# Attention's reciprocal sums through DRAM and a multiplication on GpSimd

## The chip, the core and the metric

The kernel runs on one core of a Trainium2 chip. The core has engines that run beside each other, each in its own fixed order: TensorE (PE, matmuls and transposes; PEld is its loading of weights), VectorE (DVE), ScalarE (ACT), GpSimd (POOL) and SyncE (SP). An instruction that waits holds up all that stands behind it on its engine. PE writes to PSUM, eight banks of 512 numbers in each of 128 partitions; DVE and ACT read it. DMA transfers are issued by an engine's queue (here SP and POOL above all) and then run by themselves.

The metric is the device time of one execution in microseconds (us): the median of 3 runs of the kernel before is 2940.63 us (2940.21 to 2942.37).

## The reference

Two layers over 1024 latent tokens and 256 context tokens of width 1024, in float32: a convolution module, then grouped-query attention, each followed by a SwiGLU network. The change touches the attention of the second layer alone. It has 16 heads of 64 numbers, and 4 heads of keys and values, each shared by 4 query heads; latent tokens read all 1280 tokens:

```python
def gqa_sdpa(q, k, v):
    B, Q, H, Dh = q.shape
    qg = q.reshape(B, Q, N_KV_HEADS, KV_GROUP, Dh)
    s = jnp.einsum("bqkgd,bskd->bkgqs", qg, k).astype(jnp.float32) * (Dh ** -0.5)
    p = jax.nn.softmax(s, axis=-1).astype(v.dtype)
    o = jnp.einsum("bkgqs,bskd->bqkgd", p, v)
    return o.reshape(B, Q, H * Dh)
```

The output of all heads is then multiplied by the matrix wo (the output projection), normalised, and added to the stream.

## The kernel before

Everything is laid out with features in the partitions and tokens in the free dimension. Products that need float32 accuracy are made of three matmuls: weights and inputs are each split into a rounded high part and the rest, the low part (`split`, L158 to L164: ACT copies the high part at L161, DVE subtracts at L164).

Attention is cut into 32 **units**: 4 key heads (t) times 8 blocks of 128 queries (qt); a unit has 4 query heads. The first 16 units are the first half of the tokens, the last 16 the second half.

- `scores` (L1105): for each of the 4 heads, 6 matmuls (L1116) give 128 x 1280 scores in PSUM; DVE scales them and takes the extreme (L1122); ACT takes the exponential in SBUF and adds up its row sums (L1124). There is room for two heads' scores in PSUM where attention runs alone, for one elsewhere.
- `values` (L1128): for each of 10 blocks of 128 keys, PE transposes the four heads' probabilities (L1134), ACT casts them to a high part (L1137), DVE subtracts the low part (L1138), and two matmuls (L1140, L1141) add them up in one PSUM bank, "av". Then DVE takes the reciprocals of the sums (L1145, 128 queries x 4 heads); POOL spreads each over 64 columns (L1147); ACT copies and DVE adds the two parts of the output (L1151, L1152); PE turns the spread reciprocals so that queries lie in the free dimension (L1155, two transposes into the next "av" bank, which is the same one, bank 7); DVE multiplies (L1156); POOL stores the result to the DRAM tile `od` (L1450). The last unit of each half is kept in SBUF (`olast`) and not stored.
- `attn_stream` (L1160) writes a unit's scores and the values of the unit before it in turns, as a generator. A unit's q is loaded by POOL one unit ahead (`load_q`, L1102), the keys of a head by POOL (`load_k`, L1095).

`attention` (L1430) writes the first half's units, at the start beside the projections of the last queries, then alone. The second half's stream goes into a background queue (`bgq`), and `pump` writes as much of it as its credit allows: during the output projection of the first half 0.4 of each step's us, during the first pass of the feed-forward network 0.95. `out_proj` (L1481) allocates the input tile o, loads it from `od` with four DMAs (L1485), splits it (L1489 to L1491), and then makes eight output tiles of 24 matmuls (L172 to L174).

The order on each engine is not the order of the code: a scheduler arranges the instructions by priority, which rises with the place in the code; `later` gives an instruction a later place. Buffers come from pools; where a tile gets the tag of an earlier one, it waits until that one was last used. "T" in the profile's rows stands for the tiles with the tags T1 to T6.

Of the kernel before, what the change touches and what calls it, by code (L numbers as in the profile page):

```python
# [8 lines left out]
F32 = mybir.dt.float32  # L9
# [3 lines left out]
ALU = mybir.AluOpType  # L13
AX = mybir.AxisListType

P = 128
# [4 lines left out]
TOK = CTX + SEQ  # L21
# [3 lines left out]
NH, NKV, HD = 16, 4, 64  # L25
# [30 lines left out]
class Kern:  # L56
# [1071 lines left out]
    def values(self, t, Ps, sums, dst, done):  # L1128
        nc, c = self.nc, self.c
        av = self.bank("av")  # L1130
        for j in range(NJ):
            tp = self.bank("pt")
            for h in range(4):
                nc.tensor.transpose(tp[:, h * P:(h + 1) * P], Ps[h][:, j * P:(j + 1) * P], c["ident"])  # L1134
            ph, pl = self.ptring[self.ptslot % len(self.ptring)]
            self.ptslot += 1
            nc.scalar.copy(ph, tp)  # L1137
            nc.vector.tensor_tensor(pl, tp, ph.bitcast(F32), op=ALU.subtract)  # L1138
            with self.later(self.lav):
                nc.tensor.matmul(av, lhsT=self.value(t, j), rhs=ph, start=j == 0, stop=False)  # L1140
                nc.tensor.matmul(av, lhsT=self.value(t, j), rhs=pl, start=False, stop=j == NJ - 1)  # L1141
            yield 0.87

        r = sums[:, 1, :]
        nc.vector.reciprocal(r, sums[:, 0, :])  # L1145
        rx = self.sb(256)
        nc.gpsimd.tensor_copy(rx.rearrange("p (h d) -> p h d", d=HD), r.unsqueeze(2).to_broadcast([P, 4, HD]))  # L1147
        tmp = self.sb(256).rearrange("p (a q) -> p a q", q=P)
        v = av.rearrange("p (a b q) -> p a b q", b=2, q=P)
        for b, r, o in ((0, slice(0, 64), slice(64, 128)), (1, slice(64, 128), slice(0, 64))):  # L1150
            nc.scalar.copy(tmp[r], v[o, :, b, :])  # L1151
            nc.vector.tensor_tensor(dst[r], v[r, :, b, :], tmp[r], op=ALU.add)  # L1152
        rb = self.bank("av")
        for a in range(2):
            nc.tensor.transpose(rb[:, a * P:(a + 1) * P], rx[:, a * P:(a + 1) * P], c["ident"])  # L1155
        nc.vector.tensor_tensor(dst, dst, rb[:, 0:256].rearrange("p (a q) -> p a q", q=P), op=ALU.mult)  # L1156
        done()
        yield 0.1

# [270 lines left out]
    def attention(self, final, qr):  # L1430
        nc, a, c = self.nc, self.a, self.c
        kbuf = self.T("T3", [P, 2 * TOK], F32R)
        pr1 = self.T("T1", [P, 3, TOK])
        prh = self.T("HS", [P, 4, TOK])
        ptt = self.T("T2", [P, 4, 2, 512], F32R)
        self.ptring = [(ptt[:, i, 0], ptt[:, i, 1]) for i in range(4)]
# [6 lines left out]
        def dst(q0):  # L1443
            def of(t, q):
                if (t, q % 4) == (NKV - 1, 3):
                    return self.olast, lambda: None
                st = self.sb(256).rearrange("p (a q) -> p a q", q=P)

                def done():
                    nc.gpsimd.dma_start(self.od[:, 2 * t:2 * t + 2, q * P:(q + 1) * P], st)  # L1450
                return st, done
            return of
# [11 lines left out]
        pr4 = None  # L1464
        for us in self.attn_stream(units, (self.kub, kbuf), dst(0), True):
            if self.bgq:
                self.pump(self.rate * us)
            elif pr4 is None:
                pr4 = self.T("T5", [P, 3, TOK])
                self.pring = self.pring[:4] + [pr4[:, 0], pr4[:, 1], pr4[:, 2]] + self.pring[4:]  # L1470
                self.set_banks(**alone)
                self.sring = [0, TOK]
# [8 lines left out]
        def out_proj(q0, otag, tags, ytag, box, xtag):  # L1481
            o = self.T(otag, [P, KT, 512])
            for q in range(4):
                n = 512 if q < 3 else 3 * P
                nc.gpsimd.dma_start(o[:, 2 * q:2 * q + 2, :n], self.od[:, 2 * q:2 * q + 2, q0:q0 + n])  # L1485
            oh = self.T(tags[0], [P, KT, 512], F32R)
            ol = self.T(tags[1], [P, KT, 512], F32R)
            for k in range(KT - 2):
                self.split(oh[:, k, :], ol[:, k, :], o[:, k, :])  # L1489
            self.split(oh[:, KT - 2:, :3 * P], ol[:, KT - 2:, :3 * P], o[:, KT - 2:, :3 * P])  # L1490
            self.split(oh[:, KT - 2:, 3 * P:], ol[:, KT - 2:, 3 * P:], self.olast)  # L1491
            yield 12
            y = self.T(ytag, [P, KT, 512])
            yacc = self.acc(512)
            box.append((y, yacc))

            xr = self.T(xtag, [P, KT if q0 else KT + 1, 512])
            last = self.T("HV", [P, 512]) if q0 else xr[:, KT, :]
            for q in range(0, KT, 2):
                nc.gpsimd.dma_start(xr[:, q:q + 2, :], self.x2d[:, q:q + 2, CTX + q0:CTX + q0 + 512])  # L1500
            more = [self.acc(512), last]
            box += [more, xr]
            for k in range(KT):
                o = self.bank("mm")
                self.proj(o, a["wo"][k], self.pairs(oh, ol), 512)
                nc.scalar.copy(y[:, k, :], o)  # L1506
                self.sq_acc(yacc, y[:, k, :], k)
                g = self.col[1][0][1][:, k:k + 1]
                w, p = (self.sm(512) for _ in range(2)) if k else more
                nc.scalar.activation(w, y[:, k, :], AF.Square, scale=g)  # L1510
                nc.vector.scalar_tensor_tensor(out=p, in0=y[:, k, :], scalar=g, in1=xr[:, k, :],
                                               op0=ALU.mult, op1=ALU.mult)
                if k:
                    for m, t in zip(more, (w, p)):
                        nc.vector.tensor_tensor(m, m, t, op=ALU.add)
                yield 5.1
        yL, yR, fL, fR, zL, zR = [], [], [], [], [], []
        for us in out_proj(0, "HS", ("T6", "T3"), "T4", yL, "HS"):
            self.pump(0.4 * us)
# [6 lines left out]
        def tail_R():  # L1526
            self.set_banks(mm=[0, 1, 2, 3], st=[5, 6])
            yield from out_proj(512, "T1", ("T2", "T5"), "T1", yR, "HR")
            yield from self.post_pre2(yR, self.xv[1], self.bank("st"), self.x3d[:, :, 512:], ("T2", "T5"), fR, True)
# [21 lines left out]
        yacc, n = self.acc(CTX), CTX  # L1551
# [172 lines left out]
```

## Time and profile before

The profiled execution took 2938.98 us, of which 2937.2 lie between its first and last instruction (the span).

| | us | share of the span | instructions |
|---|---|---|---|
| span of the profiled execution | 2937.2 | | 42731 |
| the profiled execution's own time | 2938.98 | | |
| median of 3 runs | 2940.63 | | |
| PE busy | 2847.7 | 97% | 16462 |
| DVE busy | 2160.7 | 74% | 3746 |
| ACT busy | 1335.5 | 45% | 2229 |
| POOL busy (with its DMA issues) | 222.6 | 8% | 377 |

Attention's values run from 1588.5 us (the first transpose of L1134) to 2393.7 us (the last multiplication of L1156). A row of a group names line, engine, operation, out<-in, the count, then the busy time and the mean duration in ns, and behind the second bar the idle time of the engine just before these instructions with what ended it. A row of a timeline has start, duration, engine and line; where it was idle before, the last bracket says how long and what it waited for. The chain is followed back from the last instruction, at each step to what released it.

### The profile page before, as it was taken

To read this page: it belongs to the slowest core of one execution; us is meant where nothing else is said; L and a number is where in the kernel's file an instruction comes from. 1 tells how busy PE (TensorE), PEld (TensorE's weight loads), DVE (VectorE), ACT (ScalarE), POOL (GpSimd) and SP (SyncE) were. 2 spreads that over 40 slices of the span, in tenths; PEclk is the share of its full clock that TensorE was granted. 3 is DMA by queue.
4 is the path that set the end of the run, shared out by engine and by line. 5 is a ranking of instruction groups with operands and counts; after the bars stand their busy time and mean duration, and the time that the engine had idled before them with its cause. 6 is when DMAs were issued, how large, how long until landed. Compare 5 with 4: busy or idle time off the path is not lost.

```text
span 2937.2 us, 42731 instructions
## 1 busy us (share of the span) xinstructions
PE 2847.7 (97%) x16462; PEld 2446.1 (83%) x16462; DVE 2160.7 (74%) x3746; ACT 1335.5 (45%) x2229; POOL 222.6 (8%) x377
## 2 busy tenths in 40 slices
PE   7999989999999999999999999989999999999998
PEld 6888877888888889989888787767777778889997
DVE  6887788847556378877786899786666666786777
ACT  5222255532222245544445688645555543444444
POOL 0000001011022001000011111110000000010000
PEclk9999999999999999999999999999999999999999
DMA  6443444334356224333345211322222143353332
GB/s 249 140 120 98 116 131 145 135 116 143 115 175 198 65 74 165 114 104 112 109 156 170 88 46 46 97 87 81 66 73 83 60 149 99 110 170 104 102 98 75
DMA packets 131755, 336.58 MB, mean 115 GB/s; under 512 B 31328, under 2 KB 52864, under 8 KB 130656
## 3 DMA queue, kind: packets, MB, share of 16 engines
q1 hardware_dynamic: 78016, 222.33, 24.1%
q0 software_dynamic: 29344, 103.83, 10.7%
q10 hardware_dynamic: 24192, 7.70, 1.1%
q8 instruction: 129, 2.11, 0.3%
q14 instruction: 74, 0.61, 0.1%
HBM read 289.50 MB, written 38.93 MB: 112 GB/s over the span
## 4 chain that ended last, share of the span: by engine, by line
PE 86%; DVE 7%; ACT 2%; issue 2%; DMA 2%; ACTq 0%; POOL 0%; SPq 0%; DVEq 0%; POOLq 0%
PE ps L172 15%; PE ps L173 15%; PE ps L174 15%; PE ps L875 4%; PE ps L877 4%; PE ps L876 4%; PE ps L1116 4%; PE ps L1134 4%; PE ps L1140 2%; PE ps L454 2%; PE ps L455 2%; PE ps L456 2%; PE ps L1141 2%; PE ps L185 1%; PE ps L183 1%
## 5 line engine op out<-in xcount | busy, mean ns | idle before, releaser
L172 PE MATMUL ps<-T,wh 128*128 128x512 f32 (+1 forms) x1360 | 502.5, 370 | 1.4 <-ACT T L161 0.8
L174 PE MATMUL ps<-T,wl 128*128 128x512 f32 (+1 forms) x1360 | 500.4, 368 | 2.0 <-DVE wl L148 2.0
L173 PE MATMUL ps<-T,wh 128*128 128x512 f32 (+1 forms) x1312 | 481.4, 367 | 0.2 <-DVE T L164 0.2
L144 ACT CAST wh<-wr 128x1024 fp32r<-128x1024 f32 (+1 forms) x217 | 225.0, 1037 | 419.9 <-PE ps L173 307.2
L148 DVE TENSOR_TENSOR wl<-wr,wh 128x1024 fp32r<-128x1024 f32 (+1 forms) x217 | 261.9, 1207 | 168.5 <-ACT wh L144 167.1
L875 PE MATMUL ps<-T,wh 128*128 128x256 f32 x1092 | 310.7, 285 | 5.0 <-ACT wh L161 4.5
L876 PE MATMUL ps<-T,wh 128*128 128x256 f32 x1092 | 306.5, 281 | 0.0
L877 PE MATMUL ps<-T,wl 128*128 128x256 f32 x1092 | 305.4, 281 | 0.2 <-DVE wl L164 0.2
L1138 DVE TENSOR_TENSOR T<-ps,T 128x512 fp32r<-128x512 f32 x320 | 216.8, 687 | 107.6 <-ACT T L1137 106.8
L172 PEld LDWEIGHTS ps<-T,wh 128*128 128x128 f32 x1360 | 257.8, 190 | 43.7 <-ACT T L1506 1.7
L174 PEld LDWEIGHTS ps<-T,wl 128*128 128x128 f32 x1360 | 257.7, 190 | 42.4 <-DVE wl L148 2.2
L173 PEld LDWEIGHTS ps<-T,wh 128*128 128x128 f32 x1312 | 248.5, 189 | 38.2 <-DVE T L164 1.3
L1137 ACT CAST T<-ps 128x512 fp32r<-128x512 f32 x320 | 186.0, 586 | 191.1 <-PE ps L1134 177.6
L173 PE MATMUL ps<-HS,wh 128*128 128x512 f32 x656 | 257.9, 393 | 0.0
L172 PE MATMUL ps<-HS,wh 128*128 128x512 f32 x608 | 238.4, 392 | 0.9 <-ACT wh L144 0.9
L174 PE MATMUL ps<-HS,wl 128*128 128x512 f32 x608 | 237.5, 391 | 0.0
L875 PEld LDWEIGHTS ps<-T,wh 128*128 128x128 f32 x1092 | 206.1, 189 | 11.2 <-ACT wh L161 6.7
L876 PEld LDWEIGHTS ps<-T,wh 128*128 128x128 f32 x1092 | 206.6, 189 | 0.5
L877 PEld LDWEIGHTS ps<-T,wl 128*128 128x128 f32 x1092 | 206.2, 189 | 0.6 <-DVE wl L164 0.4
L1134 PE MATMUL ps<-cst,T 128*128 128x128 f32 x1100 | 189.6, 275 | 3.2 <-DVE T L1138 3.1
L1122 DVE TENSOR_SCALAR_CACHE_REDUCE T<-ps,rq 128x1280 f32<-128x1280 f32 x110 | 170.0, 1546 | 27.9 <-PE ps L1116 22.1
L1134 PEld LDWEIGHTS ps<-cst,T 128*128 128x128 f32 x1100 | 132.6, 141 | 49.5 <-DVE T L1138 30.8
(377 smaller groups left out, 6195.9 us busy)
## 6 DMA issues: line engine op xcount, KB each, us to landing
wr<-in_w SPq DMA_DIRECT2D x170, 512.0 KB, 3.6
wr<-in_pw SPq DMA_DIRECT2D x35, 512.0 KB, 3.5
HV<-in_wmodT POOLq DMA_DIRECT2D x56, 256.0 KB, 4.1
q<-in_wmodT POOLq DMA_DIRECT2D x56, 256.0 KB, 3.9
KB<-in_w SPq DMA_DIRECT2D x24, 512.0 KB, 3.6
HR<-in_w SPq DMA_DIRECT2D x23, 512.0 KB, 3.7
q<-in_w SPq DMA_DIRECT2D x23, 512.0 KB, 4.2
q<-qsd POOLq DMA_DIRECT2D x32, 256.0 KB, 3.3
```

What stands on the lines that cost most here:

```text
L144: nc.scalar.copy(hi, raw)
L148: nc.vector.tensor_tensor(lo, raw, hi.bitcast(F32), op=ALU.subtract)
L172: nc.tensor.matmul(out[:, :n], lhsT=wh, rhs=xh, start=k == 0, stop=False)
L173: nc.tensor.matmul(out[:, :n], lhsT=wh, rhs=xl, start=False, stop=False)
L174: nc.tensor.matmul(out[:, :n], lhsT=wl, rhs=xh, start=False, stop=k == nk - 1)
L875: nc.tensor.matmul(out, lhsT=wh, rhs=bh, start=first and k == 0, stop=False, **skip)
L876: nc.tensor.matmul(out, lhsT=wh, rhs=bl, start=False, stop=False, **skip)
L877: nc.tensor.matmul(out, lhsT=wl, rhs=bh, start=False, stop=k == 3, **skip)
L1122: nc.vector.tensor_scalar(out=pt, in0=sc, scalar1=rq[:, h:h + 1], scalar2=None, op0=ALU.mult, op1=ALU.min, accum_out=mn)
L1134: nc.tensor.transpose(tp[:, h * P:(h + 1) * P], Ps[h][:, j * P:(j + 1) * P], c["ident"])
L1137: nc.scalar.copy(ph, tp)
L1138: nc.vector.tensor_tensor(pl, tp, ph.bitcast(F32), op=ALU.subtract)
```

## The change

Three things are changed.

1. The reciprocals are taken at the beginning of `values`, when the unit's sums are ready. POOL writes them to a DRAM tile, transposed (heads x queries, so 512 numbers of 4 bytes each), and reads them back with two DMAs that repeat each row over 64 partitions, into a tile rb of 128 x 256. Two such tiles are used in turn; they lie behind the probabilities in T1 and T5, which are 256 columns longer for it. While attention runs beside the projections, there is only the one in T1.
2. The output is multiplied by rb on POOL. The copy that spread the reciprocals, the two transposes and DVE's multiplication are gone.
3. In the output projection of the first half, the four loads of o are issued by SP and not by POOL, and 30 us of credit stand between them and the split.

```diff
     def values(self, t, Ps, sums, dst, done):
         nc, c = self.nc, self.c
         av = self.bank("av")
+        r = sums[:, 1, :]
+        nc.vector.reciprocal(r, sums[:, 0, :])
+        rd = self.rsd[self.unit]
+        rb = self.rbs[self.unit % len(self.rbs)]
+        self.unit += 1
+        nc.gpsimd.dma_start(rd.rearrange("h q -> q h"), r)
+        rv = rd.rearrange("(a b) q -> b a q", b=2)
+        for b in range(2):
+            nc.gpsimd.dma_start(rb[b * HD:(b + 1) * HD], rv[b:b + 1].to_broadcast([HD, 2, P]))
         for j in range(NJ):
...
-        r = sums[:, 1, :]
-        nc.vector.reciprocal(r, sums[:, 0, :])
-        rx = self.sb(256)
-        nc.gpsimd.tensor_copy(rx.rearrange("p (h d) -> p h d", d=HD), r.unsqueeze(2).to_broadcast([P, 4, HD]))
         tmp = self.sb(256).rearrange("p (a q) -> p a q", q=P)
...
-        rb = self.bank("av")
-        for a in range(2):
-            nc.tensor.transpose(rb[:, a * P:(a + 1) * P], rx[:, a * P:(a + 1) * P], c["ident"])
-        nc.vector.tensor_tensor(dst, dst, rb[:, 0:256].rearrange("p (a q) -> p a q", q=P), op=ALU.mult)
+        nc.gpsimd.tensor_tensor(dst, dst, rb, op=ALU.mult)
         done()
...
     def attention(self, final, qr):
...
-        pr1 = self.T("T1", [P, 3, TOK])
+        def place(tag):
+            t = self.T(tag, [P, 3 * TOK + 2 * P])
+            return t[:, :3 * TOK].rearrange("p (i n) -> p i n", i=3), t[:, 3 * TOK:].rearrange("p (a q) -> p a q", q=P)
+        pr1, rb = place("T1")
+        self.rbs, self.unit = [rb], 0
+        self.rsd = self.dp.tile([2 * NKV * 4, 4, P], F32, tag="rsd", name="rsd")
...
-                pr4 = self.T("T5", [P, 3, TOK])
+                pr4, rb = place("T5")
+                self.rbs.append(rb)
...
             for q in range(4):
                 n = 512 if q < 3 else 3 * P
-                nc.gpsimd.dma_start(o[:, 2 * q:2 * q + 2, :n], self.od[:, 2 * q:2 * q + 2, q0:q0 + n])
+                eng = nc.gpsimd if q0 else nc.sync
+                eng.dma_start(o[:, 2 * q:2 * q + 2, :n], self.od[:, 2 * q:2 * q + 2, q0:q0 + n])
+            if not q0:
+                yield 30
```

In the changed file the lines of `values` are renumbered: L1134 becomes L1143 (transposes), L1137 L1146 (casts), L1140 and L1141 become L1149 and L1150, L1151 becomes L1156 (copies), L1450 L1457 (store), L1485 L1494 (loads of o); new are L1136 (write of the reciprocals), L1139 (the broadcast loads) and L1158 (POOL's multiplication). The order moves in three places that matter below.

The first is PE, where attention runs alone, around the end of a unit's values. Before (KB holds the keys, HV and HR the values, the numbered T tiles the probabilities and their transposes):

```order
L1116 MATMUL ps<-KB,q 128x256 x2
L1116 MATMUL ps<-KB,q 128x512
L1155 MATMUL ps<-cst,sb 128x128 x2
L1116 MATMUL ps<-KB,q 128x512 x2
L1134 MATMUL ps<-cst,T_13569 128x128
L1134 MATMUL ps<-cst,T_14068 128x128 x2
L1140 MATMUL ps<-T_13571,HV 128x512
L1141 MATMUL ps<-T_13571,HV 128x512
```

The change, at the same place:

```order
L1116 MATMUL ps<-KB,q 128x256 x2
L1116 MATMUL ps<-KB,q 128x512
L1149 MATMUL ps<-T_13572,HV 128x512
L1150 MATMUL ps<-T_13572,HV 128x512
L1149 MATMUL ps<-T_13572,HV 128x512
L1143 MATMUL ps<-cst,T_13569 128x128
L1143 MATMUL ps<-cst,T_14072 128x128 x3
```

The two transposes of reciprocals are gone, and the next unit's value matmuls stand where they stood, ahead of the rest of the score matmuls. Before, the values of every second unit of this stage ended after two of the four heads of scores two units on, and those of the others after one; with the change all of them end after two.

The second is POOL, in the same stage; `q<-qsd` is the load of q, `od<-sb` the store of a unit. Before, two units:

```order
L1147 COPY sb<-sums 128x256 x2
L1450 DMA od<-sb 128x2x128
L1102 DMA q<-qsd 128x4x128 x2
L1450 DMA od<-sb 128x2x128
L1147 COPY sb<-sums 128x256 x2
```

The change, two units:

```order
L1136 DMA rsd<-sums 128x4x1
L1139 DMA T_13569<-rsd 64x2x128 x2
L1102 DMA q<-qsd 128x4x128
L1158 TENSOR_TENSOR sb<-sb,T_14072 128x256
L1457 DMA od<-sb 128x2x128
L1136 DMA rsd<-sums 128x4x1
L1139 DMA T_14072<-rsd 64x2x128 x2
L1102 DMA q<-qsd 128x4x128
L1158 TENSOR_TENSOR sb<-sb,T_13569 128x256
L1457 DMA od<-sb 128x2x128
```

Per unit there are three more DMA issues, and the broadcast loads stand behind the write that they wait for. The multiplication behind them is that of the unit before (the other of the two tiles). One row of the kind ISA stands ahead of the first multiplication of all.

The third is ACT at the join of the two halves: `T<-HS` is the high part of the split of o, `sb<-ps` the copies of a unit's output (the first two belong to the last unit that is stored). Before:

```order
L1151 COPY sb<-ps 64x256
L1137 CAST T_13571<-ps 128x512
L1151 COPY sb<-ps 64x256
L1137 CAST T_13571<-ps 128x512
L161 CAST T_15974<-HS 128x512 x4
L1137 CAST T_13571<-ps 128x512 x2
L161 CAST T_15974<-HS 128x512 x2
L1137 CAST T_13571<-ps 128x512 x2
L161 CAST T_15974<-HS 128x2x384
```

The change:

```order
L1156 COPY sb<-ps 64x256
L161 CAST T_16081<-HS 128x512
L1146 CAST T_13572<-ps 128x512
L1156 COPY sb<-ps 64x256
L1146 CAST T_13572<-ps 128x512
L161 CAST T_16081<-HS 128x512 x2
L1146 CAST T_13572<-ps 128x512
L161 CAST T_16081<-HS 128x512
L1146 CAST T_13572<-ps 128x512
L161 CAST T_16081<-HS 128x512 x2
L1146 CAST T_13572<-ps 128x512 x3
L161 CAST T_16081<-HS 128x2x384
```

Although the split is written later in the code, it stands at nearly the same place: the first piece has moved ahead of two casts and a copy, the last one is one cast later. On SP the four loads of o stand behind the loads of the first five weights of the projection and ahead of the others.

## The prediction

> **What bounds the kernel now.** I read the page first, then the stretches of the attention stage, then the chain of work that ended last, inside two of them.
>
> ```profile
> PE 2847.7 (97%) x16462; PEld 2446.1 (83%) x16462; DVE 2160.7 (74%) x3746; ACT 1335.5 (45%) x2229; POOL 222.6 (8%) x377
> PE 86%; DVE 7%; ACT 2%; issue 2%; DMA 2%; ACTq 0%; POOL 0%; SPq 0%; DVEq 0%; POOLq 0%
> ```
>
> TensorE (PE) carries 86% of the chain and GpSimd (POOL) none of it. So an instruction taken from PE is worth its own length wherever PE never waits, and work given to POOL is free as long as nobody waits for POOL. The busy time by stretch says where that holds; the columns are the stretch, its length, then PE, PEld, DVE, ACT and POOL busy.
>
> ```profile
> 1660.00:1840.00 180.00, 174.77 (x1052) 143.18 (x1051) 164.71 (x270) 147.09 (x248) 25.91 (x42) 1.00 0.19 49
> 1840.00:1880.00 40.00, 37.15 (x198) 28.86 (x198) 33.52 (x55) 29.96 (x51) 9.12 (x13) 1.00 0.42 135
> 2000.00:2380.00 380.00, 379.96 (x1958) 298.76 (x1957) 250.89 (x368) 207.19 (x323) 27.21 (x43) 1.00 0.26 76
> ```
>
> In 1660 to 1840 the first half of the attention runs alone: 12 units in 180 us, 15 us each, with PE and DVE both nearly full. From 2000 to 2380 most of the second half runs beside the feed-forward network: PE is idle for 0.04 us, and DVE for 129 us. Between them lies the join (1840 to 1880), where the output projection starts. The chain inside the two long stretches, by line (the two pieces of rows below are in this order):
>
> ```profile
> by line: PE ps L1134 20.1%; PE ps L1116 18.2%; PE ps L1140 14.1%; PE ps L1141 13.1%; DVE T L1138 9.8%; issue 7.4%; DVE T L1122 5.1%; ACT T L1137 4.1%; DVE HS L1122 3.6%; DVE sb L1152 2.4%; PE ps L1155 1.5%; ACT sb L1151 0.5%; ACT T L1124 0.
> ```
> ```profile
> by line: PE ps L173 17.2%; PE ps L172 17.2%; PE ps L174 17.2%; PE ps L1134 15.4%; PE ps L1116 15.4%; PE ps L1140 8.5%; PE ps L1141 8.1%; PE ps L1155 1.1%; issue 0.0%
> ```
>
> L1155, the two transposes that the change removes, is on the chain in both. L1156, DVE's multiplication, is in neither.
>
> **Transposes beside the network.** One pair seen close, as start, duration, operation:
>
> ```profile
> 2188.96 0.40 PE L1116 MATMUL ps<-KB,q 128*128 128x256 f32 x2
> 2189.20 0.41 PE L1155 MATMUL ps<-cst,sb 128*128 128x128 f32 x2
> 2189.36 0.71 PE L1116 MATMUL ps<-KB,q 128*128 128x512 f32 x2
> 2189.91 0.49 PE L1134 MATMUL ps<-cst,T 128*128 128x128 f32 x3
> ```
>
> Matmuls overlap, so starts count, not durations. The pair holds PE from 2189.20 to 2189.36, 0.16 us, and the two 512-wide matmuls behind it take 0.55 us, where they would take 0.48 (the first row has two 256-wide ones, as much as one 512-wide, in 0.24): 0.23 us in all. The chain gives more: 1.1% of 380 us is 4.2 us for the 13 pairs in that stretch, 0.32 us each. I take 0.32 (it is measured over 13, not one) and keep 0.23 and 0.41 (the pair's whole duration) as ends. All 16 pairs of the second half lie where PE is full: 16 x 0.32 = **5.1 us less** (3.7 to 6.6).
>
> **First half.** By the chain a pair costs 1.5% of 180 us over 12, 0.225 us. DVE also loses a multiplication:
>
> ```profile
> L1138 DVE TENSOR_TENSOR T<-ps,T 128x512 fp32r<-128x512 f32 x122 | 81.1, 685 | 12.0 <-ACT T L1137 11.7
> L1152 DVE TENSOR_TENSOR sb<-ps,sb 64x256 f32<-64x256 f32 x25 | 10.4, 416 | 0.4
> L1156 DVE TENSOR_TENSOR sb<-sb,ps 128x256 f32<-128x256 f32 x12 | 4.9, 410 | 0.0
> L1145 DVE RECIPROCAL sums<-sums 128x4 f32<-128x4 f32 x12 | 2.1, 173 | 2.7 <-ACT T L1124 2.7
> ```
>
> These are 0.41 us per unit. DVE's rows hold 20.9% of this stage's chain (9.8 + 5.1 + 3.6 + 2.4), but not L1156 itself, so I count a fifth, 0.085, with 0 and 0.41 as ends. The reciprocal only moves: it already waits for the last exponential (2.7 us over 12), and stands in the same gap. So 0.225 + 0.085 = 0.31 per unit, over 16 units **5.0 us less**. The upper end is 16 x 0.635 = 10.2. The lower is 0, because the order of a unit changes: every unit now has the pattern that only every second had (the PE rows in the section on the change), DVE waits 11.7 us on ACT's copies here, and a new order can lose as much as the pair gave. Late next in this stage is that wait, L1138 on L1137, and the score matmuls on DVE's L1122.
>
> **The DRAM trip and GpSimd's multiplication.** They add, per unit, three DMA issues and one two-input operation on POOL, and remove a copy:
>
> ```profile
> L1102 POOL DMA_DIRECT2D q<-qsd x32 | 24.6, 769 | 319.9 <-PE ps L1116 311.5 <-PE ps L1134 5.7 <-DVE wl L148 1.8
> L1450 POOL DMA_DIRECT2D od<-sb x30 | 21.6, 721 | 160.7 <-DVE sb L1156 139.4 <-DVE sums L1145 20.0 <-issue 1.2
> L1147 POOL COPY sb<-sums 128x256 f32<-128x256 f32 x32 | 13.8, 432 | 73.1 <-issue 25.6 <-PE ps L1134 23.2 <-DVE sums L1145 18.7
> q<-qsd POOLq DMA_DIRECT2D x32, 256.0 KB, 3.3
> od<-sb POOLq DMA_DIRECT2D x30, 128.0 KB, 2.6
> ```
>
> An issue costs POOL 0.72 to 0.77 us. The multiplication is not in the trace: between 0.41 (DVE's L1156, the same shape) and 0.86 (the copy twice, once per input); I take 0.8. POOL's row per unit (the second piece of order) is: write the sums' reciprocals 0.72, wait for them to land (L), two broadcast loads 1.44, load q 0.77, multiply the unit before 0.8, store it 0.72. That is 4.45 us + L. The load of the sums is not multiplied with until a whole row later, so only the write's landing counts. With 2.6 to 3.3 us for L, POOL needs 7.8 us of a 15 us unit: hidden, **0 us**. It blocks no one: behind the wait stand the broadcast, then the load of q (used a unit later), then the store. The cover is 15 us less 4.45, so it is gone at an L of about 10.5 us. Beside the network a unit has 29 us (380 over 13), and more cover. A one-time row on POOL ahead of the first multiplication has no time in the trace; it stands in a row that has nothing else to do, so 0, at most one unit.
>
> **The join.** The loads of the split's input go from POOL's queue to SP's, and 30 us of credit at 0.4 (12 us of second-half work) is emitted before the split. The order shows little of that: ACT's splits hardly move: the first stands two casts and a copy earlier, the last one cast later (the third piece). Now:
>
> ```profile
> 1848.28 2.16 POOL L1485 DMA_DIRECT2D HS<-od  x3 [5.14 <-PE ps L1134]
> 1850.55 0.37 ACT L1151 COPY sb<-ps 64x256 f32<-64x256 f32 x1
> 1852.81 1.14 ACT L161 CAST T<-HS 128x512 fp32r<-128x512 f32 x2
> 1860.72 0.83 ACT L161 CAST T<-HS 128x768 fp32r<-128x768 f32 x1 [2.05 <-DMA HS<-od]
> 1862.09 0.50 PE L1140 MATMUL ps<-T,HR 128*128 128x512 f32 x1 [1.18 <-ACT T L1137]
> ```
>
> ACT waits 2.05 us for the last load, and PE 1.18 us for ACT: at most 2 us to gain, and the load still follows a store that now follows POOL's multiplication. The first split moves from 1852.81 to behind the copy that ends at 1850.92, while its load, issued at 1848.28, lands 3.3 (as q) or more later, at 1851.6 or after: ACT waits 0.7 us or more there, up to 3 us if all three loads must land. I take 0.5 us **more**, from 2 less to 3 more. SP has the weights of five output tiles issued ahead of these loads, so it holds up none that is near.
>
> **Sum.** 5.1 + 5.0 - 0.5 = 9.6 us less. The profiled execution took 2938.98 us (2937.2 from first to last instruction), so 2929.4; the median of the runs is 1.65 us above it: **2931 us**. With all ends at their best 6.6 + 10.2 + 2 = 18.8, so 2922; at their worst 3.7 + 0 - 3 = 0.7, so 2940.
>
> **Rivals.** (1) *The new order eats the first half's gain.* For it: DVE's 11.7 us of waits on ACT are not touched, and PE's idle time there (5 us of 180) is small, so PE's and DVE's orders decide. Against it: L1155 itself is on that chain. Then only 5.1 - 0.5 = 4.6 remain: 2936. (2) *Slower: the write of reciprocals binds POOL.* It writes 512 pieces of 4 bytes, and no transfer in the trace is cut like that. If L passes 10.5 us, each unit of the lone stage (14, from 1640 to 1850) lengthens by the excess: with L at 13 us, 14 x 2.5 = 35 us more, less 4.6, about 2971. Against it stands the queues' time per packet:
>
> ```profile
> q0 software_dynamic: 29344, 103.83, 10.7%
> q10 hardware_dynamic: 24192, 7.70, 1.1%
> ```
>
> 16 engines x 2937 us x 10.7% over 29344 packets is 0.17 us a packet (3.5 KB), and 0.02 us on q10 (0.3 KB). 512 pieces over 16 engines are 32 each: 0.7 to 5.5 us on top of 2.6, so L is 3.3 to 8.1, under 10.5. [...] (3) *The split isn't really later.* The order already shows this; then the join is 0 and not -0.5, and the time is 2930.5, the forecast's own.
>
> **How the numbers follow.** Forecast with rival 3, 0.63; rival 1, 0.24; rival 2, 0.13. A run of this kernel can tell 0.2%, 5.9 us, from no change; of the forecast's range little (0.03) lies above 2934.7. So faster 0.60, same 0.27, slower 0.13. The range takes the forecast's ends and rival 1, and leaves out rival 2 and a little on each side: 2922 to 2942.
>
> **What would show it.** Right: no L1155, 14 to 15 us per unit of the lone stage and about 0.3 less than now, the write landing in 3 to 8 us, a multiplication under 0.9 us, and the stretch beside the network some 5 us shorter. Wrong: POOL on the chain, PE or ACT waiting for a load of q, new ACT waits on HS above 3 us, or DVE waits on L1137 grown by more than 5 us in the lone stage.

## The result, and the profile after

| | us |
|---|---|
| the kernel before, median of 5 runs on the same chip | 2940.5 (2939.13 to 2942.37) |
| the changed kernel, median of 5 runs | 2961.97 (2956.75 to 2963.0) |
| ratio, with its 95% interval | 1.0073 (1.0062 to 1.0084) |
| span of the profiled execution after | 2960.2 (before 2937.2) |

The change makes the kernel 21 us slower. 2931 was predicted, with a range that ended at 2942. The page of the changed kernel, its busy times and the chain by engine:

```profile
PE 2852.3 (96%) x16398; PEld 2448.6 (83%) x16398; DVE 2151.1 (73%) x3714; ACT 1336.3 (45%) x2229; POOL 293.3 (10%) x469
PE 83%; DVE 9%; ACT 3%; DMA 3%; issue 2%; POOL 0%; ACTq 0%; SPq 0%; DVEq 0%; POOLq 0%
```

64 transposes are gone, and yet PE is busy for 4.6 us more (a halved clock, as will be seen) and idle for 18.4 us more (2960.2 - 2852.3 against 2937.2 - 2847.7). POOL still has no part in the chain; DMA has 1 point more. The same three stretches as in the prediction, after the change:

```profile
1660.00:1840.00 180.00, 172.39 (x1024) 140.80 (x1025) 160.14 (x260) 148.33 (x245) 54.96 (x80) 1.00 0.29 59
1840.00:1880.00 40.00, 29.60 (x160) 23.43 (x159) 27.95 (x45) 24.43 (x45) 8.11 (x12) 0.91 0.26 70
2000.00:2380.00 380.00, 378.06 (x1937) 299.33 (x1936) 248.01 (x358) 208.07 (x325) 55.24 (x80) 1.00 0.37 82
```

In the lone stage DVE is busy for 4.6 us less and PE for 2.4 less. In the join PE lost 7.6 us in 40, and its clock fell to 0.91. The timeline of the join says why, by engine: POOL's write of the reciprocals and its next issue, then SP's loads of o, ACT's first split, and PE's transposes.

```profile
1848.90 0.77 POOL L1136 DMA_DIRECT2D rsd<-sums  x1 [0.96 <-DVE sums L1132]
1858.79 1.20 POOL L1139 DMA_DIRECT2D T<-rsd  x2 [9.12 <-DMA rsd<-sums]
1851.17 17.81 SPq L1494 DMA_DIRECT2D HS<-od  x4
1862.77 0.62 ACT L161 CAST T<-HS 128x512 fp32r<-128x512 f32 x1 [8.49 <-DMA HS<-od]
1864.78 1.12 PE L1143 MATMUL ps<-cst,T 128*128 128x128 f32 x4 [8.97 <-DVE T L1147]
```

The loads were issued at 1851, while the write was under way, and ACT stood 8.49 us at the head of its queue for the first of them. The attention's casts are queued behind that split, DVE waited 8.48 us for it at L164, ahead of its own share of those casts, and PE stood still for 8.97 us. The list of DMA issues in 1845 to 1870 (transfer, count, size, median time to landing), before and after, shows how late the loads were:

```profile
HS<-od POOLq DMA_DIRECT2D x3, 512.0 KB, 5.3
```
```profile
HS<-od SPq DMA_DIRECT2D x3, 512.0 KB, 12.4
rsd<-sums POOLq DMA_DIRECT2D x1, 2.0 KB, 9.6
```

Behind the output projection TensorE's clock is halved for longer. The windows of 10 us around the norm, before and after; the third number from the right is the granted clock:

```profile
1930.00:1940.00 10.00, 8.94 (x50) 7.08 (x50) 8.08 (x24) 3.87 (x7) 0.00 (x0) 0.83 0.19 61
1940.00:1950.00 10.00, 2.85 (x14) 1.81 (x14) 9.82 (x30) 1.07 (x2) 2.80 (x6) 0.72 0.27 105
1950.00:1960.00 10.00, 8.87 (x30) 6.67 (x31) 10.00 (x16) 4.08 (x6) 0.69 (x2) 0.77 0.14 52
```
```profile
1960.00:1970.00 10.00, 9.07 (x35) 7.36 (x35) 5.53 (x18) 2.71 (x5) 1.21 (x2) 0.51 0.53 88
1970.00:1980.00 10.00, 4.47 (x15) 2.98 (x15) 9.16 (x31) 1.07 (x2) 2.22 (x4) 0.50 0.26 99
1980.00:1990.00 10.00, 7.83 (x24) 5.49 (x23) 10.00 (x16) 4.08 (x6) 1.08 (x2) 0.63 0.21 79
```

Taken 1 us at a time the granted clock there is 1.00 or 0.50, and something between only where it changes (after, it is 0.50 in each us from 1961 to 1987). So what a window's mean lacks to 1 is read as time at half the clock, twice as long as what it lacks: 2 x 10 x (0.17 + 0.28 + 0.23) = 13.6 us before and 2 x 10 x (0.49 + 0.50 + 0.37) = 27.2 us after. This is not the loss, because PE also waits in it. Within the halved time PE was busy for 7.85 us before (1934.22 to 1937.63 and 1944.46 to 1954.70) and for 18.69 us after (1960.10 to 1987.41); half of the difference, 5.4 us, is an estimate of what the longer halved clock costs here.

To find where the 23 us between the two spans come from, the start of every instruction that two kernels share was compared (engine, line, names and number of occurrence); the table gives the median shift against the kernel before, in us, around five points of its time. A kernel with credit does attention work earlier, so its column 1960 does not compare with that of the others; its columns 1840, 2440 and 2520 do.

```
                                  1580   1840   1960   2440   2520
the change                         3.3    3.6   31.0   18.8   23.3
parts 1 and 2 alone                1.4   -0.2   11.0    5.9    7.4
the change without the credit     -1.7   -2.8    7.0    1.6    3.2
  the same, rows of 16 bytes       2.4    1.6    6.2    1.3    2.8
part 3 alone                      -1.5   -1.6   15.8    7.8   14.4
only the loads on SP's queue      -2.7   -1.2    1.0    0.1    1.6
new way in the second half only    0.4   -0.5    1.6   -3.7   -1.8
no division at all                -1.0   -1.4    1.4   -1.4   -1.4
```

So the changed kernel's profile is 3.3 us late before the first new instruction runs (a stretch of halved clock, in the last section), gains nothing in the lone stage, loses 15.2 us from 1840 to 2440 and 4.5 us more at the second norm. From 2520 on nothing changes.

### The profile page after: what moved, and what is told of

It is laid out like the page before. It is cut to its first block, busy times and chain, and to the rows that moved or that the text cites. A ratio compares the mean times of both kernels' runs of the same rounds, so it can differ in the third digit from the quotient of the medians.

```text
span 2960.2 us, 42637 instructions
## 1 busy us (share of the span) xinstructions
PE 2852.3 (96%) x16398; PEld 2448.6 (83%) x16398; DVE 2151.1 (73%) x3714; ACT 1336.3 (45%) x2229; POOL 293.3 (10%) x469
## 4 chain that ended last, share of the span: by engine, by line
PE 83%; DVE 9%; ACT 3%; DMA 3%; issue 2%; POOL 0%; ACTq 0%; SPq 0%; DVEq 0%; POOLq 0%
PE ps L172 14%; PE ps L174 14%; PE ps L173 14%; PE ps L875 4%; PE ps L877 4%; PE ps L876 4%; PE ps L1116 4%; PE ps L1143 3%; PE ps L454 2%; PE ps L456 2%; PE ps L455 2%; PE ps L1149 2%; PE ps L1150 2%; PE ps L185 1%; PE ps L184 1%
## 5 line engine op out<-in xcount | busy, mean ns | idle before, releaser
L148 DVE TENSOR_TENSOR wl<-wr,wh 128x1024 fp32r<-128x1024 f32 (+1 forms) x217 | 261.9, 1208 | 167.9 <-ACT wh L144 167.3
L1146 ACT CAST T<-ps 128x512 fp32r<-128x512 f32 x320 | 185.8, 585 | 193.1 <-PE ps L1143 180.9
L1143 PE MATMUL ps<-cst,T 128*128 128x128 f32 x1100 | 188.5, 277 | 11.1 <-DVE T L1147 11.1
L1122 DVE TENSOR_SCALAR_CACHE_REDUCE T<-ps,rq 128x1280 f32<-128x1280 f32 x110 | 170.0, 1545 | 26.5 <-PE ps L1116 20.3
L1143 PEld LDWEIGHTS ps<-cst,T 128*128 128x128 f32 x1100 | 134.1, 142 | 56.6 <-DVE T L1147 38.3
```

The costliest lines, as they stand in the source:

```text
L148: nc.vector.tensor_tensor(lo, raw, hi.bitcast(F32), op=ALU.subtract)
L1122: nc.vector.tensor_scalar(out=pt, in0=sc, scalar1=rq[:, h:h + 1], scalar2=None, op0=ALU.mult, op1=ALU.min, accum_out=mn)
```

## The experiments

Times are medians, in brackets the ratio to the kernel before, run beside it, with its 95% interval.

**The parts apart.** First parts 1 and 2 without part 3:

```diff
-                eng = nc.gpsimd if q0 else nc.sync
-                eng.dma_start(o[:, 2 * q:2 * q + 2, :n], self.od[:, 2 * q:2 * q + 2, q0:q0 + n])
-            if not q0:
-                yield 30
+                nc.gpsimd.dma_start(o[:, 2 * q:2 * q + 2, :n], self.od[:, 2 * q:2 * q + 2, q0:q0 + n])
```

> Parts 1 and 2 of the change alone: the loads of o stay on GpSimd's queue and no credit stands ahead of the split. Theory A (the write of 512 pieces of 4 bytes slows the loads of o, ACT stands at the head of its queue for them, TensorE runs dry and its clock is halved afterwards): here the loads stand on GpSimd behind the wait for a write and the two broadcast loads, so they start some 8 us later than before the change but clear of the write; ACT waits 5 to 9 us on them, 2953 to 2962 us. Rival B (the move of the loads to SP's queue and the 30 us of credit cost the time, the write costs nothing): the loss is gone, 2930 to 2941 us. Rival C (the new order of TensorE's work in the attention costs it, stage by stage): 2955 to 2962 us, but with ACT's wait on HS under 3 us.

Measured: 2946.7 us (1.0025, 1.0016 to 1.0035). Below theory A's range, above rival B's; ACT waited 8.8 us as A said. Then part 3 alone, on the kernel before (the same lines, the other way round):

> Part 3 alone, on the kernel before: loads of o from SP's queue, 30 us of credit ahead of the split, reciprocals by transposes as before. Theory A: no write of small pieces is in the queues, the loads land in 3.5 to 6 us, ACT waits under 3 us for them, 2935 to 2944 us. Rival B: 2950 us or more, with ACT's wait on HS 5 us or more. Rival C: as the kernel before, 2938 to 2943 us, since the attention's order is that of before.

Measured: 2953.29 us (1.0045, 1.003 to 1.0059), with ACT's wait for HS at 2.1 us in all. So part 3 costs 12.8 us without any write of reciprocals and without a late load: theory A misses this, and B has the size but the wrong place. Alone, the parts cost 6.2 us (parts 1 and 2) and 12.8 us (part 3), 19.0 of the 21.5 that they cost together.

**The write's pieces.** The changed kernel, with the write cut in another way:

```diff
-        nc.gpsimd.dma_start(rd.rearrange("h q -> q h"), r)
+        nc.gpsimd.dma_start(rd.rearrange("h (p x) -> (h p) x", x=4), r)
```

> The changed kernel with the reciprocals written as 128 rows of 16 bytes, one a partition, in place of 512 pieces of 4 bytes; every other instruction and its order is the same. The broadcast then reads the reciprocals of other queries and heads, so the division of the attention's output by its sums is changed. Theory A: the write lands in 3 to 5 us where it took 9.8, the loads of o in 4 to 6 us where they took 12.4, ACT's wait of 8.5 us falls under 3 us, and 10 to 17 us of the 21 come back: 2945 to 2952 us. Rivals B and C: the landing falls too, but the time stays within 2956 to 2963 us.

Measured: 2954.18 us (1.0046, 1.0031 to 1.0061): 7.8 us come back, less than theory A wanted, more than B and C allow. The write landed in 1.8 us (median of 32), the loads of o in 7.2, and ACT's longest wait was 2.8 us.

**The credit.** The changed kernel without it:

```diff
-            if not q0:
-                yield 30
```

> The changed kernel without the 30 us of credit ahead of the split; the loads of o stay on SP's queue. Theory A: the first split still stands on ACT behind the same casts and the loads still meet the write, so ACT waits 7 us or more and the time is within 2954 to 2963 us. Rival B in the form that the credit costs the time: 2940 to 2950 us. Rival C: 2955 to 2962 us.

Measured: 2944.94 us (1.0015, 1.0005 to 1.0024), 17 us less than with it, and this although ACT's wait is what it was (these are the waits in 1840 to 2000: engine and line, what ended them, us in total, times, longest):

```profile
PE ps L1143 <- DVE T L1147: 9.6, 2, 9.2
ACT T L161 <- DMA HS<-od: 8.7, 1, 8.7
```

So the stall at the join, which the profile shows best, is the smaller cost; the credit, which shows as no wait at the join, is the larger. The next runs tell these two apart. Without the credit, and with rows of 16 bytes:

> The changed kernel without the credit, and with the reciprocals written as 128 rows of 16 bytes (which changes the division by the sums, as in the run with such rows before). Theory A now: the change holds two costs that add up, the write of small pieces (8 us, from the runs with the credit) and the credit (13 to 17 us). Then this run stands 6 to 9 us below the run without the credit: 2935 to 2939 us, with the loads of o landing in 4 to 7 us and ACT's wait on them under 4 us. Rival: the pieces cost something only together with the credit (which sets the phase in which the loads are met): 2943 to 2947 us.

Measured: 2942.58 us (1.0005, 0.9996 to 1.0013), 2.4 us less than with the pieces, where theory A wanted 6 to 9: nearer to the rival. The waits in the same stretch:

```profile
ACT T L161 <- DMA HS<-od: 4.1, 2, 3.1
PE ps L1143 <- DVE T L1147: 4.2, 3, 3.6
```

The profiles give more than the medians: from 1840 to 2440 the table of shifts has 4.4 us with pieces and -0.3 with rows, 4.7 apart. The pieces cost 2 to 5 us without the credit, then, and 8 with it. Then the queue alone, on the kernel before:

```diff
-                nc.gpsimd.dma_start(o[:, 2 * q:2 * q + 2, :n], self.od[:, 2 * q:2 * q + 2, q0:q0 + n])
+                eng = nc.gpsimd if q0 else nc.sync
+                eng.dma_start(o[:, 2 * q:2 * q + 2, :n], self.od[:, 2 * q:2 * q + 2, q0:q0 + n])
```

> The kernel before with the loads of o on SP's queue, and nothing else. The queue of the loads is no cost: 2936 to 2943 us. If SP's queue is a part of what part 3 costs (12.8 us): 2946 us or more.

Measured: 2940.89 us (1.0001, 0.9992 to 1.001). SP's queue costs nothing; part 3's cost is the credit. That gave theory Q, a price for each us of attention placed ahead of the split, tried with `yield 60`:

> Part 3 alone with 60 in place of 30 us of credit. Theory Q (each us of attention placed ahead of the split costs, since the network then lacks it as filling): twice the loss of part 3 alone, 2962 to 2970 us. Theory P (the credit shifts in which phase of an attention unit the output projection ends; the norm's chain then stands behind a unit's score work or not, and the clock is halved for longer or not): no such growth, anywhere from 2938 to 2957 us, and the time goes with the length of the halved clock after the output projection (13.6 us in the kernel before, 27.3 with 30 us of credit).

Measured: 2964.32 us (1.0079, 1.0065 to 1.0093), 23.4 us where 30 us cost 12.8, as theory Q said. And the credit taken down instead:

```diff
-            yield 12
+            yield 12 if q0 else 1
```

> The kernel before with the loads of o on SP's queue, and the 12 us of credit that it has behind the split taken down to 1 us: 11 x 0.4 = 4.4 us less attention ahead of the first output tile. Theory Q (30 and 60 us more cost 12.8 and 23.4 us, so 0.4 us for each us of credit, in both directions): 4 to 5 us less than with the queue alone, 2934 to 2938 us. Theory R (only credit beyond what the kernel before has costs): 2938 to 2944 us.

Measured: 2957.13 us (1.0055, 1.0041 to 1.0069). Theory Q falls, and theory R with it: less credit costs as well. And half the credit of part 3 (`yield 15`):

> Part 3 alone with 15 us of credit in place of 30. Theory Q: half the loss, 2945 to 2949 us. Theory P (the phase in which the output projection ends): 2938 to 2944 or 2950 us and more.

Measured: 2939.4 us (0.9993, 0.9984 to 1.0001), no cost at all. Two points that lay on a line were not a law. All five on the kernel before with SP's queue, with the halved time worked out as above from the clock of 1920 to 2010, PE's idle time from 2000 to 2560 (the stretches of these windows less PE's busy time), and what PE waited for there:

| credit against before | time against before, us | clock halved, us | PE idle, us | PE's waits over 1 us |
|---|---|---|---|---|
| 11 less | +15.3 | 27 | 7.2 | wl 3.3, KB 2.5 |
| the same | -0.1 | 14 | 0.5 | none |
| 15 more | -2.4 | 20 | 1.3 | none |
| 30 more | +12.8 | 27 | 6.7 | wl 2.9, KB 1.1, olast 1.2, issue 1.1 |
| 60 more | +23.4 | 23 | 9.0 | wl 5.0, T 1.6, T 1.1 |

(In the last column, "issue" is time in which PE waited for nothing that the profile shows.) Two things go together in the three that lose and are absent in the other two: the low part of the next weights (wl, L148 on DVE) comes 2.9 to 5.0 us too late at the second norm, and PE is idle for 7 to 9 us. Loads of keys (KB) that land too late when the head changes show in two of the three (2.5 and 1.1 us; 0.4 with 60 more). The clock is halved for longer around the first norm in all three, but this length alone does not sort the runs: 20 us went with no loss, 23 us with the largest.

All five have the same 16462 matmuls, so the difference of two spans can be divided into PE's busy and idle time over the whole execution. Against the kernel before, 30 more has 9.3 us more busy and 4.5 more idle, 60 more 13.6 and 12.4, and 11 less 8.9 and 10.7; 15 more has 1.0 and -1.1. The same matmuls took longer at a lower mean clock (0.984, 0.983 and 0.983 granted, where the kernel before has 0.987). So, as an estimate, the halved clock makes about half of the loss (45 to 67%), and waits make the rest.

These are rows of PE's waits in the changed kernel, from 2000 to 2400 and from 2480 to 2560; the kernel before has neither:

```profile
PE ps L1116 <- DMA KB<-ksd: 1.7, 2, 1.3
```
```profile
PE ps L174 <- DVE wl L148: 2.6, 2, 1.8
```

Last, the changed kernel with 15 us of credit:

> The changed kernel with 15 us of credit in place of 30. Theory P (what counts is where in a unit the credit lets the output projection end, as in the kernel before: 15 us more cost nothing, 30 and 60 more and 11 less cost 12 to 23): 17 us come back almost whole, 2942 to 2948 us, with a halved clock of 14 to 21 us around the first matmul of the network. Theory Q' (in the changed kernel the loss grows with the credit): half of it, 2951 to 2956 us.

Measured: 2948.61 us (1.0028, 1.0016 to 1.0041): 13.4 of the 17 us come back (12.5 if each kernel is set against the kernel before that ran beside it), 0.6 us outside theory P's range and 2.4 outside that of Q'. Its clock is halved for 20 us, and it has neither the wait for wl nor more than 0.5 us for KB.

**The gain.** The kernel before with nothing in place of the division:

```diff
-        rx = self.sb(256)
-        nc.gpsimd.tensor_copy(rx.rearrange("p (h d) -> p h d", d=HD), r.unsqueeze(2).to_broadcast([P, 4, HD]))
...
-        rb = self.bank("av")
-        for a in range(2):
-            nc.tensor.transpose(rb[:, a * P:(a + 1) * P], rx[:, a * P:(a + 1) * P], c["ident"])
-        nc.vector.tensor_tensor(dst, dst, rb[:, 0:256].rearrange("p (a q) -> p a q", q=P), op=ALU.mult)
```

> The kernel before without the division by the sums: no spread copy, no transposes of it, no multiplication (this leaves a part of the computation out). It has what the change removes and nothing of what it adds. If the gain of the first half (5.0 us in the prediction) is there and the trip through DRAM or GpSimd eats it: the lone stage is 3 to 8 us shorter than before. If TensorE's new order eats it, as in rival 1 of the prediction: the lone stage is within 1 us of before, and the stretch beside the network 4 to 6 us shorter. Whole run 2930 to 2937 us.

Measured: 2938.82 us (0.9993, 0.9984 to 1.0001), above the range. From 1660 to 1840 its shift changes by 0.1 us, as expected with rival 1. From 1960 to 2440 it changes by -2.8, less than the 4 to 6 expected with it, and from 1840 to 1960 as much is lost. Even with everything removed and nothing added there was hardly a gain to be had: 3.0 us, and 4.7 at most by the interval. The two rows of the lone stage that answer to those of before, for this kernel and for the changed one:

```profile
L1138 DVE TENSOR_TENSOR T<-ps,T 128x512 fp32r<-128x512 f32 x123 | 80.1, 684 | 15.4 <-ACT T L1137 15.0
```
```profile
L1147 DVE TENSOR_TENSOR T<-ps,T 128x512 fp32r<-128x512 f32 x122 | 79.5, 684 | 15.6 <-ACT T L1146 15.2
```

In both, DVE waits 3.3 to 3.5 us longer for ACT's casts than before (11.7), and PE is idle for 7.6 to 7.8 us in 180 where it was 5.2.

**A better version.** The new way for the second half's units only (`self.unit > 16`), loads on SP's queue, no credit:

```diff
+        trip = self.unit > 16
+        if trip:
+            nc.vector.reciprocal(r, sums[:, 0, :])
+            nc.gpsimd.dma_start(rd.rearrange("h q -> q h"), r)
...
+        if trip:
+            nc.gpsimd.tensor_tensor(dst, dst, rb, op=ALU.mult)
+        else:
...
```

> The new way (reciprocals through DRAM, GpSimd multiplies) for the second half's 16 units only, the first half as before; loads of o on SP's queue, no credit. The first write then comes after the loads of o. Theory A: the join is as in the kernel before (ACT's wait for HS under 3 us), and the 16 pairs of transposes beside the network are saved: 3 to 6 us less than the kernel before, 2934 to 2938 us. Rival: the small pieces slow the loads beside the network as well and eat the gain: 2939 to 2944 us.

Measured: 2937.93 us (0.9989, 0.998 to 0.9998), 3 us less than the kernel before: the fastest of all, by little. The loads landed in 4.9 us and ACT waited 0.9. With 11 us of credit less, and with 15 more:

> The new way for the second half's units only, as before, with the same 11 us of credit taken away. Theory Q: 4 to 5 us under the run of the second half alone (2937.9), 2932 to 2935 us. Theory R: 2935 to 2941 us.

> The new way for the second half's units only, loads on SP's queue, 15 us of credit. Theory P: what 15 us of credit gave on the kernel before (2.4 us under the kernel before) and what the second half gives (3.0 us under it) lie in different stages and add up at most: 2934 to 2939 us. If the phase is lost with the new order of the second half: 2945 us or more.

Measured: 2954.92 us (1.0046, 1.0034 to 1.0059) and 2938.96 us (0.9999, 0.999 to 1.0007). The first lies above both of its ranges, so less credit costs here as well; in the second the two small gains don't add up.

## Why the prediction was wrong

- **Transposes beside the network** (5.1 less, 3.7 to 6.6): borne out in the profiles, near the lower end. From 1960 to 2440 the four kernels with the new way and no credit gain 4.9 to 5.4 us in the table of shifts. The control with nothing but the queue moved gains 0.9 there, which leaves 4.0 to 4.5. The run without any division has lost the same transposes and gains only 2.8 there, with PE idle for 1.1 us of 2000 to 2380 where it was 0.04. In the medians, the new way in the second half alone gained 3.0 us (0.6 to 5.9 by the interval).
- **First half** (5.0 less, 0 to 10.2): wrong in the value, and the lower end came true. Between 1660 and 1840 the shift changes by 0.3 us at most in any run of the table (what changes between 1580 and 1840 lies at 1640 or before, in stretches of halved clock; the one at 1640 lasts from 0 to 6.8 us, depending on the run). The step that failed: the share of L1155 on the chain, and a fifth of the multiplication, were taken as savings. The order of a unit changes, and what was saved came back as waiting: PE is busy for 2.4 us less in 1660 to 1840 and idle for as much more, and DVE waits for the casts longer. This is rival 1's outcome, and the run without any division shows it without the trip through DRAM. The sign I named for it (5 us more of that wait) was set too high: 3.5 were enough.
- **The trip and GpSimd's multiplication** (hidden, 0): right for POOL, and closer than thought. The multiplication took 747 ns (0.8 taken); the write's landing was off, 9.8 us where 3.3 to 8.1 were the bounds. These rows are the write's and the multiplication's in the changed kernel, with the landing's least, middle and longest time:

```profile
L1136 POOL DMA_DIRECT2D rsd<-sums x32: 750/767/820, 1608.4 to 2368.6; - x32
DMA to landing us min/median/max: 8.6/9.8/11.8
```
```profile
L1158 POOL TENSOR_TENSOR sb<-sb,T x30: 724/747/763, 1650.6 to 2369.4; 128x256 f32<-128x256 f32 x30
```

  4.45 + 9.8 is 14.2 us of a unit of 15. Rival 2's mechanism, POOL as the bound, did not come; but the same pieces hit what I never priced, the other transfers in the queues.
- **The join** (0.5 more, from 2 less to 3 more): the step that failed most, and twice. The loads were taken to land as q does, in 3.3 us, with "up to 3 us if all three loads must land", though these very loads had landed in 5.3 us in the kernel before. Beside the write they took 12.4 us, and ACT waited 8.49 us, which is one of the signs that I had named for being wrong (new waits on HS above 3 us). Of that the pieces make 2.4 us without the credit and 7.8 with it (medians). And the credit was judged by where the splits stand on ACT ("the order shows little of that"). What it changed lay behind the output projection, where I had not looked: the halved clock, the loads of keys and the second norm. Without it the changed kernel is 17 us faster. In the profiles, the 0.5 us that was taken for the join stands against some 24 us: 15.2 from 1840 to 2440, the 4 to 4.5 saved in between, and 4.5 at the second norm.
- **Rival 3** (the split isn't really later): the splits hardly moved in ACT's order, as said, but its price for the credit, nothing, was wrong by those 17 us.

Summed in the profiles, the changed kernel lost 3.3 us before its first new instruction, 0.3 in the lone stage, 15.2 from 1840 to 2440 (net of the 4 to 4.5 saved) and 4.5 at the second norm: 23.3 of the 23.0 between the spans.

Three things stay open. The first is what it is in the phase that decides: five credits show that the time jumps by 13 to 23 us and with what it goes together, but not by which unit boundary, and no run held the halved clock fixed. The second is why DVE's wait grows in the lone stage: the run without division has the shorter order too, so the order was not tried apart from the removed work. The third is where the pieces hold up the loads beside them; the runs show that they do and by how much.

## What to carry to other kernels

An instruction's share of the chain need not be a saving where the order around it changes: in the lone stage all of it came back as waiting. Leaving the operation out altogether tells early what there is to gain, and here that was some 3 us. The narrow transfer had two prices here, its own landing (9.8 us) and that of the loads it met (12.4 us in place of 4.7), and only the first was in the sum. Where work is interleaved by credit, try values on both sides: 30 and 60 us more made a straight line, and 11 less and 15 more showed that there was none.

## What the runs showed of the hardware

512 pieces of 4 bytes landed in 9.8 us (8.6 to 11.8), and the same 2 KB as 128 rows of 16 bytes in 1.8 us (1.7 to 5.8 without the credit). Three loads of 512 KB took 4.7 to 4.9 us from SP's queue with no write beside them, 7.2 beside rows of 16 bytes, and 11.7 to 12.6 beside pieces of 4. The count of packets does not show where the difference comes from: from 1700 to 1900 the changed kernel's profile has 1392 under 512 B with 12 writes in pieces, the same kernel with rows of 16 bytes 1312 with 11 writes, and part 3 alone, which has none, 592. Put down to the writes alone, that is 65 to 67 for each either way, and what differs is the landing.

TensorE's clock was halved (0.50 or 0.51 in each us from 1565 to 1571) in a stretch before the attention in which the code is the same and PE hardly paused. These are rows of PE and a window of the changed kernel:

```profile
1562.48 0.38 PE L1015 MATMUL ps<-cst,sm 128*128 128x4 f32 x2 [0.78 <-ACT sm L1008]
...
1568.01 0.63 PE L173 MATMUL ps<-T,wh 128*128 128x512 f32 x1
1568.43 0.63 PE L174 MATMUL ps<-T,wl 128*128 128x512 f32 x1
...
1571.22 0.40 PE L172 MATMUL ps<-T,wh 128*128 128x512 f32 x1
1571.46 0.40 PE L173 MATMUL ps<-T,wh 128*128 128x512 f32 x1
```
```profile
1560.00:1575.00 15.00, 14.22 (x57) 11.56 (x56) 7.93 (x14) 5.41 (x8) 0.75 (x2) 0.77 0.34 113
```

Matmuls of 512 columns start 0.42 us apart at 1568 and 0.24 apart at 1571; 2 x 15 x 0.23 = 6.9 us of halved clock make the 3.2 us by which this profile is late from there on (a median shift of 0.1 us around 1560, 3.3 around 1575). In the 9 us before this stretch PE was never idle for more than 0.8 us, and what halved the clock there the trace does not show. The 16 profiles of this case have the same code in this stretch, and from 1545 to 1580 the mean clock is 1.00 in 7 of them, 0.95 in 3 and 0.90 in 6, which is 0, 3.5 or 7 us of halved clock. So a few us between two profiles can be the clock's alone, and medians of several runs were needed here.
